# Chunk attention on one Trainium2 core: probabilities by values as three float32r products of high and low parts

## The chip, the cores and the metric

The kernel runs on one core of a Trainium2 chip. The metric is the time of one execution on the device in microseconds (us); the number given for a kernel is the median of several executions. The profile is of one execution, whose own time stands beside it.

## What is computed

Two layers of a streaming encoder, x of 256 frames by 2048 features. Each layer has three groups of heads from one input projection: chunk attention (8 heads of 128), gated linear attention (4 heads), attention into 256 memory tokens (4 heads). The change touches the chunk attention alone:

```python
scores = jnp.einsum('bnqhd,bnkhd->bnhqk', qc, k_band) * (Dh ** -0.5)
scores = jnp.where(valid, scores + bias, NEG_INF)
p = jax.nn.softmax(scores, axis=-1)
out = jnp.einsum('bnhqk,bnkhd->bnqhd', p, v_band)      # probabilities by values
...
y = jnp.concatenate([y_a * silu(a_z), y_b * silu(b_z), y_m * silu(m_z)], axis=-1)
x = layer_norm(alpha * x + y @ w_out, ln_g, ln_b)
```

With 256 frames in chunks of 64 and eight chunks to the left, each frame attends to all frames up to the end of its own chunk. The kernel works in two halves of 128 frames: the first half sees keys 0 to 127, the second keys 0 to 255. So one head's probabilities by values are a product over keys 0 to 127 for all 256 frames (128 x 256) and one over keys 128 to 255 for the second 128 frames (128 x 128).

## The kernel before, in words

**Weights and products.** All projections are a stream of weight pieces (128 x 1024 floats as a rule, 128 x 528 in a part of the value projection). `piece` (L140) loads one into `raw`, and `parts` (L126) splits it: ScalarE (ACT) copies it to float32r, `wh`, and VectorE (DVE) subtracts that from `raw` for the rest, `wl`. TensorE (PE) then makes three float32r products for each of four pairs of k-tile and frame half (`as_products`, L258): high by high, low by high, high by low, twelve matmuls a piece. `raw`, `wh` and `wl` have four buffers each (pool `wp`, L86), so the `wh` of a piece reuses the buffer of the piece four before, and its cast can start only when PE has read that one.

**Attention heads.** `a_head` (L540) is a generator. It issues query by key products as plain float32 matmuls into a PSUM bank, adds the bias and takes the maximum on DVE, the exponential on ACT, scales by the reciprocal sum on DVE, and hands the probabilities `s` to `turned` (L520), which transposes 32 x 32 blocks on DVE and goes through DRAM by POOL's DMA queue into `pT`. Then it yields 9 units of time, and after that issues the values product: two plain float32 matmuls from `asv` (values) and `pT` (L566, L567), and a copy of the bank to `yr` on ACT. A plain float32 matmul appears in the profile as two PE instructions.

`m_head` (L571), the memory heads, already uses the form that the change brings to `a_head`: it splits `pT` into `ph` and `pl` by `parts(..., placed_here)`, yields 2, and issues three float32r products of 128 x 256 for each half of the memory.

**What sets the order.** `tick` (L52) is called once for each piece of weights that PE works through (a fraction of a unit for the narrow pieces). It takes steps of the generators whose time has come: heads start when one of two or three places among the active ones is free, and one step that yields is taken per tick; a generator that ends frees its place within the same tick, and the next starts at once. PE, SP (DMA queue of the weights) and POOL issue in the order in which the code is written (L49). ACT and DVE are ordered by the language's scheduler before the run: the splits of weight pieces have a high priority (`AHEAD`, 4000), and what is marked `placed_here` (L122) stays behind everything that was written before it on its engine. Each engine runs its instructions strictly in that order.

`scratch` (L107) hands out tiles from eight buffers (pool `sc`, L89).

Of the kernel before, what the change touches and what calls it, by code (L numbers as in the profile page):

```python
# [9 lines left out]
F32R = mybir.dt.float32r  # L10
# [8 lines left out]
P = 128  # L19
# [17 lines left out]
def hybrid_trunk_kernel(  # L37
# [59 lines left out]
    def nm(s):  # L97
        uid[0] += 1
        return f"{s}_{uid[0]}"

    def mm(o, l, r, start, stop):
        pe.matmul(o, l, r, start=start, stop=stop, skip_group_check=True)  # L102

    def bank():
        return psa.tile([P, 512], F32, name=nm("bk"), tag="bk")

    def scratch(shape, dtype=F32):  # L107
        return sc.tile(shape, dtype, name=nm("sc"), tag="sc")

    def small(shape, tag, bufs=1):  # L110
        return sm.tile(shape, F32, name=nm(tag), tag=tag, bufs=bufs)
# [14 lines left out]
    def parts(hi, lo, src, keep=lambda ins: ins):  # L126

        keep(act.copy(hi, src))  # L128
        keep(dve.tensor_tensor(lo, src, hi.bitcast(F32), op=ALU.subtract))  # L129
# [390 lines left out]
    def turned(n, *todo, order="p b (g j) -> p g b j"):  # L520

        homes = []
        for _, src in todo:
            blocks = scratch([P, 4, n])
            dve.transpose(blocks.rearrange(order, j=32), src.rearrange("p (g b j) -> p g b j", b=4, j=32))  # L525
            homes.append(drm.tile([P, 4, n], F32, name=nm("home"), tag=f"home{n}"))
            pool.dma_start(homes[-1], blocks)  # L527

        def reads():
            for (dst, _), home in zip(todo, homes):  # L530
                for b in range(4):
                    pool.dma_start(dst[b * 32:(b + 1) * 32], home[:, b].rearrange("(a i) n -> i a n", a=4))  # L532
            return
            yield

        side.append((reads(), now[0] + 2))
# [3 lines left out]
    def a_head(h, load_bias, bias, q, k, asv, y):  # L540

        pb = bank()
        pv = pb.rearrange("p (a j) -> p a j", j=32)
        mm(pv[:, 0:4], q[:, 0:128], k[:, 0:4], True, True)
        mm(pv[:, 4:12], q[:, 128:256], k, True, True)
        s = scratch([P, 384])
        dve.scalar_tensor_tensor(s, pb[:, :384], SCALE, bias[h], op0=ALU.mult, op1=ALU.add)  # L547
        mx = small([P, 2], "mx", 4)
        zs = small([P, 2], "zs", 4)
        own = (slice(0, 128), slice(128, 384))  # L550
        for t in range(2):
            dve.tensor_reduce(mx[:, t:t + 1], s[:, own[t]], AX.X, ALU.max, negate=True)  # L552
        for t in range(2):
            act.activation(s[:, own[t]], s[:, own[t]], AF.Exp, bias=mx[:, t:t + 1], accum_out=zs[:, t:t + 1])  # L554
        dve.reciprocal(zs, zs)
        for t in range(2):
            dve.tensor_scalar(s[:, own[t]], s[:, own[t]], zs[:, t:t + 1], None, op0=ALU.mult)
        pT = tp.tile([P, 4, 96], F32, name=nm("pT"), tag="pT")
        turned(96, (pT, s))
        yield 9  # L560
        if h < 4:
            load_bias(h + 4)
        po = bank()
        v0 = 528 + h * P
        pv, pov = pT.rearrange("p a (g j) -> p g a j", j=32), po[:, :256].rearrange("p (t a j) -> p t a j", t=2, j=32)
        mm(pov, asv[:, 0, v0:v0 + P], pv[:, 0:2], True, False)  # L566
        mm(pov[:, 1], asv[:, 1, v0:v0 + P], pv[:, 2], False, True)  # L567
        act.copy(y, po[:, :256])
        yield 2

    def m_head(h, q, mk, mv, y, laid):  # L571

# [94 lines left out]
    def wo_pieces(l, n):  # L667

        if n < 3:
            return [w512[l, G_WO + n, pc] for pc in range(8)]  # L670
        return [[w256[l, i, pc // 2][:, pc % 2 * 512:pc % 2 * 512 + 512] for i in range(2)] for pc in range(8)]
# [143 lines left out]
    for l in range(L):  # L815
# [63 lines left out]
        asv = per.tile([P, 2, 1552], F32, name=nm("asv"), tag="asv")  # L879
# [17 lines left out]
        home = drm.tile([P, 2, 64], F32, name=nm("home"), tag="home64")  # L897
# [17 lines left out]
        def load_bias(h):  # L915
            bias[h] = hd.tile([P, 384], F32, name=nm("bias"), tag="bias", bufs=4)
            sp.dma_start(bias[h], relw[l, h])
# [20 lines left out]
        for half in range(2):  # L938
            q, k = (hd.tile([P, 4, T], F32, name=nm("qk"), tag="qk", bufs=4) for _ in range(2))
            laid = staged(G_AQ0 if half == 0 else G_AQ1, xq, yraw[3], lambda src, at, q=q: placed_here(act.copy(at(q), src)))  # L940
            load_res(half * 2)
            if half == 0:
                load_bias(2)
            laid += staged(G_AK0 if half == 0 else G_AK1, xq, k, None)
            if half == 0:
                load_bias(3)
            load_res(half * 2 + 1)
            if half == 0:
                values(776, 512)
            else:  # L950
                values(1288, 264)
                mq = staged_queries()
            finish(laid)
            kv = k.rearrange("p x y -> p (x y)").rearrange("p (ta g j) -> p g ta j", g=4, j=32)
            gens.append([a_head(half * 4 + h, load_bias, bias, q[:, h], kv[:, h], asv, yraw[1 + half][:, h]) for h in range(4)])
            waiting.extend(gens[-1])
# [35 lines left out]
        for n in range(WO_N):  # L992
# [3 lines left out]
            src = wo_pieces(l, n)  # L996
# [141 lines left out]
```

## Time and profile before

| | us |
|---|---|
| median of 3 runs (897.84 to 900.17) | 899.92 |
| the profiled execution, own time | 899.75 |
| its span, first to last instruction | 898.0 |
| PE busy (matmul) | 889.1 |
| DVE busy | 613.7 |
| ACT busy | 478.0 |
| POOL busy | 230.9 |

The span is what the trace covers; 1.75 us of the execution's own time lie outside it. A matmul row's duration is from its start to its modelled end, and matmuls overlap: what a matmul costs PE is the distance from its start to the next one's start. In a timeline row, `x4` means four instructions merged, and the first number is the start of the first. "PEld" is the weight load of PE, which runs beside matmuls.

### The profile page before, as it was taken

How to read it: one execution, taken by the hardware profiler on the slowest of the kernel's cores; microseconds unless marked ns; L12 is line 12 of the kernel's file. 1: busy time of each engine (PE TensorE's matmuls, PEld its weight loads, DVE VectorE, ACT ScalarE, POOL GpSimd, SP SyncE). 2: the span in 40 equal slices, each digit the busy share in tenths (PEclk: the TensorE clock that was granted, in tenths of full speed). 3: DMA queues.
4: the chain of work that ended last, by engine and by line, in shares of the span. 5: the costliest groups of instructions: out<-in, count | busy, mean ns of one | idle time of the engine just before them, and what ended most of it. 6: DMA issues, size and time to landing. Idle time of an engine off the chain costs nothing.

```text
span 898.0 us, 13829 instructions
## 1 busy us (share of the span) xinstructions
PE 889.1 (99%) x4663; PEld 743.6 (83%) x4663; DVE 613.7 (68%) x893; ACT 478.0 (53%) x686; POOL 230.9 (26%) x431
## 2 busy tenths in 40 slices
PE   9999999999999999999999999999999999999997
PEld 7888988888988888888888788888888888888885
DVE  6766568757477666665595687896565758676766
ACT  6643574555446565543465544754744457565440
POOL 0022103114315353410033221231061334342300
PEclk9999999999999999999999999999999999999998
DMA  9987779967989797975689879697489887978752
GB/s 301 318 264 223 223 244 263 272 195 226 266 259 242 238 279 228 297 254 193 225 267 270 229 203 291 192 290 219 144 235 290 244 265 232 271 237 275 219 183 93
DMA packets 166086, 216.88 MB, mean 242 GB/s; under 512 B 25232, under 2 KB 143376, under 8 KB 166016
## 3 DMA queue, kind: packets, MB, share of 16 engines
q1 hardware_dynamic: 148256, 173.29, 63.7%
q0 software_dynamic: 17472, 42.33, 16.2%
q8 instruction: 36, 0.59, 0.3%
q10 hardware_dynamic: 288, 0.39, 0.1%
q14 instruction: 34, 0.28, 0.1%
HBM read 194.78 MB, written 21.10 MB: 240 GB/s over the span
## 4 chain that ended last, share of the span: by engine, by line
PE 71%; issue 13%; DMA 9%; DVE 3%; POOL 2%; ACT 1%; SPq 0%; DVEq 0%; POOLq 0%; ACTq 0%
PE acc L102 65%; PE bk L102 6%; DMA zT<-home 2%; DMA home<-sc 2%; DMA xT<-home 2%; DMA raw<-w 2%; DVE wl L129 1%; DMA qk<-home 1%; DMA res<-memT 1%; DMA gb<-ln_b 1%; POOL home L527 0%; POOL xT L532 0%; DMA pT<-home 0%; POOL qk L532 0%; DVE sc L525 0%
## 5 line engine op out<-in xcount | busy, mean ns | idle before, releaser
L102 PE MATMUL acc<-wh,x 128*128 128x512 f32 (+2 forms) x2516 | 748.4, 381 | 0.2 <-ACT wh L128 0.2
L102 PEld LDWEIGHTS acc<-wh,x 128*128 128x128 f32 x2516 | 460.9, 188 | 87.1 <-ACT wh L128 1.0
L129 DVE TENSOR_TENSOR wl<-raw,wh 128x1024 fp32r<-128x1024 f32 (+3 forms) x321 | 368.0, 1151 | 203.0 <-ACT wh L128 196.8
L128 ACT CAST wh<-raw 128x1024 fp32r<-128x1024 f32 (+3 forms) x321 | 318.1, 995 | 336.5 <-PE acc L102 185.7
L102 PE MATMUL acc<-wl,x 128*128 128x512 f32 (+2 forms) x1258 | 476.3, 379 | 1.4 <-DVE wl L129 1.3
L102 PEld LDWEIGHTS acc<-wl,x 128*128 128x128 f32 x1258 | 236.0, 188 | 48.1 <-DVE wl L129 3.5
L527 POOL DMA_DIRECT2D home<-sc x76 | 42.5, 560 | 436.0 <-DVE sc L525 423.1
L532 POOL DMA_DIRECT2D pT<-home x96 | 52.4, 552 | 24.8 <-PE acc L102 8.8
L532 POOL DMA_DIRECT2D qk<-home x64 | 34.9, 553 | 35.5 <-DMA home<-sc 25.2
L532 POOL DMA_DIRECT2D zT<-home x48 | 26.1, 551 | 19.0 <-DMA home<-sc 13.4
L525 DVE STREAM_TRANSPOSE sc<-sc 128x512 f32<-128x512 f32 (+1 forms) x38 | 24.9, 667 | 3.7 <-ACT sc L974 3.0
L532 POOL DMA_DIRECT2D yr<-home x48 | 26.3, 555 | 4.2 <-DMA home<-sc 3.2
L554 ACT ACTIVATE sc<-sc,mx 128x128 f32<-128x128 f32 (+1 forms) x32 | 14.4, 449 | 13.0 <-DVE mx L552 13.0
L525 DVE STREAM_TRANSPOSE sc<-acc 128x512 f32<-128x512 f32 x28 | 18.3, 690 | 4.4 <-PE acc L102 4.3
L547 DVE SCALAR_TENSOR_TENSOR sc<-bk,bias 128x384 f32<-128x384 f32 x16 | 8.6, 538 | 10.8 <-PE bk L102 10.8
L128 ACT CAST x<-sc 128x512 fp32r<-128x512 f32 x20 | 12.3, 618 | 5.3 <-DVE sc L508 2.7
L532 POOL DMA_DIRECT2D xT<-home x24 | 13.2, 552 | 6.5 <-DMA xT<-home 5.3
L129 DVE TENSOR_TENSOR x<-sc,x 128x512 fp32r<-128x512 f32 x20 | 13.5, 684 | 1.4 <-ACT x L128 1.4
L102 PEld LDWEIGHTS bk<-pT,asv 128*128 128x128 f32 x64 | 11.8, 189 | 1.8
L102 PE MATMUL bk<-qk,qk 128*128 128x128 f32 (+1 forms) x64 | 13.1, 326 | 0.0
L676 DVE SCALAR_TENSOR_TENSOR res<-res,acc 128x512 f32<-128x512 f32 x15 | 9.6, 681 | 5.0 <-PE acc L102 5.0
L102 PE MATMUL bk<-pT,asv 128*128 128x256 f32 (+1 forms) x64 | 13.0, 326 | 0.0
(208 smaller groups left out, 508.6 us busy)
## 6 DMA issues: line engine op xcount, KB each, us to landing
raw<-w SPq DMA_DIRECT2D x387, 256.0 KB, 4.6
raw<-w SPq DMA_DIRECT2D x62, 512.0 KB, 4.5
home<-sc POOLq DMA_DIRECT2D x60, 256.0 KB, 4.4
raw<-w SPq DMA_DIRECT2D x32, 388.0 KB, 5.0
raw<-w SPq DMA_DIRECT2D x32, 264.0 KB, 3.5
qk<-home POOLq DMA_DIRECT2D x64, 64.0 KB, 5.4
raw<-w SPq DMA_DIRECT2D x32, 124.0 KB, 4.9
bias<-relw SPq DMA_DIRECT2D x16, 192.0 KB, 4.3
```

What stands on the lines that cost most here:

```text
L102: pe.matmul(o, l, r, start=start, stop=stop, skip_group_check=True)
L128: keep(act.copy(hi, src))
L129: keep(dve.tensor_tensor(lo, src, hi.bitcast(F32), op=ALU.subtract))
L525: dve.transpose(blocks.rearrange(order, j=32), src.rearrange("p (g b j) -> p g b j", b=4, j=32))
L527: pool.dma_start(homes[-1], blocks)
L532: pool.dma_start(dst[b * 32:(b + 1) * 32], home[:, b].rearrange("(a i) n -> i a n", a=4))
L547: dve.scalar_tensor_tensor(s, pb[:, :384], SCALE, bias[h], op0=ALU.mult, op1=ALU.add)
L554: act.activation(s[:, own[t]], s[:, own[t]], AF.Exp, bias=mx[:, t:t + 1], accum_out=zs[:, t:t + 1])
L676: dve.scalar_tensor_tensor(r, r, ALPHA, acc, op0=ALU.mult, op1=ALU.add)
```

## The change

The generator of a head splits its 128 x 256 part of the probabilities (`pv[:, 0:2]`) and its 128 x 128 values of the first half (`asv[:, 0, ...]`) into high and low float32r parts, each pair in one scratch tile, by four more instructions that are placed in program order: two casts on ACT and two subtractions on DVE. It then yields 1 and issues three float32r products of 128 x 256 in place of one plain float32 product. The 128 x 128 part over keys 128 to 255 stays a plain float32 product. The last `yield 2` is gone: the generator ends with the product, so a head lasts 9 + 1 units where it lasted 9 + 2, and the request for the next bias comes one unit later.

```diff
         yield 9
+        v0 = 528 + h * P
+        pv = pT.rearrange("p a (g j) -> p g a j", j=32)
+        ph, pl = split(scratch([P, 512], F32R), 256, pv[:, 0:2], "p (t a j) -> p t a j", t=2, j=32)
+        vh, vl = split(scratch([P, 256], F32R), P, asv[:, 0, v0:v0 + P], "p n -> p n")
+        yield 1
         if h < 4:
             load_bias(h + 4)
         po = bank()
-        v0 = 528 + h * P
-        pv, pov = pT.rearrange("p a (g j) -> p g a j", j=32), po[:, :256].rearrange("p (t a j) -> p t a j", t=2, j=32)
-        mm(pov, asv[:, 0, v0:v0 + P], pv[:, 0:2], True, False)
-        mm(pov[:, 1], asv[:, 1, v0:v0 + P], pv[:, 2], False, True)
+        mm(po[:, :256], vh, ph, True, False)
+        mm(po[:, :256], vl, ph, False, False)
+        mm(po[:, :256], vh, pl, False, False)
+        mm(po[:, P:256].rearrange("p (a j) -> p a j", j=32), asv[:, 1, v0:v0 + P], pv[:, 2], False, True)
         act.copy(y, po[:, :256])
-        yield 2
+
+    def split(home, n, src, shape, **kw):
+
+        hi, lo = home[:, :n], home[:, n:]
+        parts(hi.rearrange(shape, **kw), lo.rearrange(shape, **kw), src, placed_here)
+        return hi, lo
```

The order that comes out of it moves at every head. Three pieces of it follow, all at the values product of the first head of the first layer; the second layer has the same rows there with other numbers. A number behind `wh_` or `wl_` (one higher) names a piece of weights; the pieces run in the order of their numbers.

PE before. `bk_2074` is the first head's values product, `acc_2002` the projection that runs around it:

```order
L102 MATMUL acc_2002<-wh_2042,x_265 128x512 x2
L102 MATMUL acc_2002<-wl_2043,x_265 128x512
L102 MATMUL bk_2074<-pT_1715,asv_686 128x256
L102 MATMUL bk_2074<-pT_1715,asv_686 128x128
L102 MATMUL acc_2002<-wh_2079,x_350 128x512 x2
L102 MATMUL acc_2002<-wl_2080,x_350 128x512
```

PE with the change, where `sc_2072` holds `ph` and `pl`, `sc_2075` holds `vh` and `vl`, and `bk_2109` is the query by key product of the fourth head:

```order
L102 MATMUL acc_2002<-wh_2079,x_350 128x512 x2
L102 MATMUL acc_2002<-wl_2080,x_350 128x512
L102 MATMUL bk_2103<-sc_2072,sc_2075 128x256 x3
L102 MATMUL bk_2103<-pT_1715,asv_686 128x128
L102 MATMUL bk_2109<-qk_1025,qk_1024 128x128
L102 MATMUL bk_2109<-qk_1025,qk_1024 128x256
L102 MATMUL acc_2002<-wh_2129,x_350 128x512 x2
```

The values product has moved one piece later, behind the piece 2079, and the fourth head's query by key product follows it at once.

ACT before. `sc_2025` are the scores of the third head, whose exponential waits for the maximum `mx_2027` from DVE; the pieces behind 2079 are 2102, 2140, 2159, 2182:

```order
L128 CAST wh_2159<-raw_2158 128x1024
L568 COPY yr_1021<-bk_2074 128x256
L128 CAST wh_2182<-raw_2181 128x1024
L554 ACTIVATE sc_2025,zs_2028<-sc_2025,mx_2027 128x128
L554 ACTIVATE sc_2025,zs_2028<-sc_2025,mx_2027 128x256
L128 CAST wh_2201<-raw_2200 128x1024
```

ACT with the change; the pieces behind 2079 are now 2129, 2148, 2171, 2190:

```order
L128 CAST wh_2171<-raw_2170 128x1024
L128 CAST wh_2190<-raw_2189 128x1024
L554 ACTIVATE sc_2025,zs_2028<-sc_2025,mx_2027 128x128
L554 ACTIVATE sc_2025,zs_2028<-sc_2025,mx_2027 128x256
L128 CAST sc_2072<-pT_1715 128x256
L128 CAST sc_2075<-asv_686 128x128
L573 COPY yr_1021<-bk_2103 128x256
```

The two casts of the split stand behind the cast of piece 2190, which takes the buffer of piece 2079, and behind the third head's exponentials.

DVE before, from the third head's maximum on (`sc_2037` are the blocks of its transposition, `sc_2123` the scores of the fourth head):

```order
L552 TENSOR_REDUCE mx_2027<-sc_2025 128x1 x2
L129 TENSOR_TENSOR wl_2183<-raw_2181,wh_2182 128x1024
L555 RECIPROCAL zs_2028<-zs_2028 128x2
L557 TENSOR_SCALAR sc_2025<-sc_2025,zs_2028 128x128
L557 TENSOR_SCALAR sc_2025<-sc_2025,zs_2028 128x256
L525 STREAM_TRANSPOSE sc_2037<-sc_2025 128x3x4x32
L547 SCALAR_TENSOR_TENSOR sc_2123<-bk_2120,bias_1422 128x384
```

DVE with the change:

```order
L552 TENSOR_REDUCE mx_2027<-sc_2025 128x1 x2
L129 TENSOR_TENSOR wl_2191<-raw_2189,wh_2190 128x1024
L555 RECIPROCAL zs_2028<-zs_2028 128x2
L557 TENSOR_SCALAR sc_2025<-sc_2025,zs_2028 128x128
L557 TENSOR_SCALAR sc_2025<-sc_2025,zs_2028 128x256
L525 STREAM_TRANSPOSE sc_2037<-sc_2025 128x3x4x32
L129 TENSOR_TENSOR sc_2072<-pT_1715,sc_2072 128x256
L129 TENSOR_TENSOR sc_2075<-asv_686,sc_2075 128x128
```

The two subtractions of the split stand where the addition of the fourth head's bias stood, behind all of the third head's softmax; the rows ahead of them are the same as before.

## Prediction

> **What bounds the kernel now.** First the page's busy times and its slices.
>
> ```profile
> PE 889.1 (99%) x4663; PEld 743.6 (83%) x4663; DVE 613.7 (68%) x893; ACT 478.0 (53%) x686; POOL 230.9 (26%) x431
> PEclk9999999999999999999999999999999999999998
> ```
>
> PE is busy for 99% of the span at the full granted clock until the last slice. Busy alone proves little, since matmuls overlap, so the second view is the list of waits of PE:
>
> ```profile
> PE acc L102 <- DVE wl L129: 1.3, 3, 0.8
> PE bk L102 <- DVE eps L814: 1.1, 1, 1.1
> PE bk L790 <- DVE nt L755: 0.9, 1, 0.9
> PE bk L102 <- ACT nparts L791: 0.3, 1, 0.3
> PE acc L102 <- ACT wh L128: 0.2, 1, 0.2
> ```
>
> This is the whole list: 3.8 us in 898. No head's product waits for anything. So the time is the sum of what PE issues, and a change pays or costs in two ways only: by the PE time of its matmuls, and by any place where PE begins to wait. A wait isn't made up later, because no stage has PE time to spare.
>
> **What the matmuls cost.** The timeline of PE around the first head's values product, and around a memory head's:
>
> ```profile
> 206.24 0.62 PE L102 MATMUL acc<-wh,x 128*128 128x512 f32 x2
> 206.69 0.39 PE L102 MATMUL acc<-wl,x 128*128 128x512 f32 x1
> 206.92 0.81 PE L102 MATMUL bk<-pT,asv 128*128 128x256 f32 x4
> 207.49 0.71 PE L102 MATMUL acc<-wh,x 128*128 128x512 f32 x2
> 208.04 0.40 PE L102 MATMUL acc<-wl,x 128*128 128x512 f32 x1
> ...
> 210.32 0.62 PE L102 MATMUL acc<-wh,x 128*128 128x512 f32 x2
> ...
> 337.78 0.89 PE L102 MATMUL bk<-sc,mv 128*128 128x256 f32 x6
> 338.51 0.63 PE L102 MATMUL acc<-wh,x 128*128 128x512 f32 x2
> ```
>
> The four instructions of the two plain products take 207.49 - 206.92 = 0.57 us, and the next triple is 0.10 late (0.55 from `wh` to `wl` instead of 0.45): 0.67 in all. By columns, two thirds are the 128x256 part, 0.45. Three float32r products of 128x256 take half of 338.51 - 337.78, or 0.36. Gain: 0.45 - 0.36 = 0.09 by rounded rows; since the 0.10 may belong to whichever product stands last, which stays, I take 0.07 and keep 0.05 to 0.09. Times 16 heads: **-1.1 us** (-0.8 to -1.4).
>
> The Trainium skill ("FP8 and Floating Point Precision", TensorE Precision Notes) counts four passes for a true float32 product. By it the change would save one pass in four, 0.12 us of these rows a head, or 1.9 us in all; the rows show less, and the sum goes by the rows.
>
> **What the split costs on ACT and DVE.** Each head adds two casts and two subtractions; the nearest rows:
>
> ```profile
> L128 ACT CAST sc<-pT 128x256 fp32r<-128x256 f32 x16 | 5.7, 405 | 1.5 <-DMA pT<-home 1.5
> L129 DVE TENSOR_TENSOR sc<-pT,sc 128x256 fp32r<-128x256 f32 x16 | 6.0, 413 | 0.1
> L496 DVE SCALAR_TENSOR_TENSOR x<-yT,ng,x 128x128 fp32r<-128x128 f32 x16 | 4.5, 345 | 0.0
> ```
>
> The 128x256 cast takes 0.41, its subtraction 0.41, the 128x128 subtraction at most 0.35, the 128x128 cast less than 0.41. So some 0.75 us per head on each engine, 12 us in all on engines that are 47% and 32% idle: nothing by itself. What counts is where in the queue they stand, since PE now waits for their result, where it read `pT` and `asv` directly before.
>
> **Where PE will wait.** In the order with the change, the first head's split stands on ACT behind the cast of piece 2190. That cast takes the buffer of piece 2079, and 2079 is the very piece that PE works through just ahead of the values product. So ACT comes to the split only when PE is already at the product. Behind that cast also stand the third head's two exponentials. Before, the cast at the same place, and the exponentials:
>
> ```profile
> 206.89 1.05 ACT L128 CAST wh<-raw 128x1024 fp32r<-128x1024 f32 x1 [0.20 <-PE acc L102]
> ...
> 210.30 1.06 ACT L128 CAST wh<-raw 128x1024 fp32r<-128x1024 f32 x1 [1.96 <-PE acc L102]
> 211.72 0.40 ACT L554 ACTIVATE sc<-sc,mx 128x128 f32<-128x128 f32 x1 [0.37 <-DVE mx L552]
> ...
> 212.52 0.19 ACT L554 ACTIVATION_READ_ACCUMULATOR sc<-sc,mx 128x1 f32 x1
> ```
>
> And DVE from that maximum on:
>
> ```profile
> 211.42 0.60 DVE L552 TENSOR_REDUCE mx<-sc 128x1 f32<-128x128 f32 x2
> 211.94 1.21 DVE L129 TENSOR_TENSOR wl<-raw,wh 128x1024 fp32r<-128x1024 f32 x1
> 213.07 0.16 DVE L555 RECIPROCAL zs<-zs 128x2 f32<-128x2 f32 x1
> 213.26 0.55 DVE L557 TENSOR_SCALAR sc<-sc,zs 128x128 f32<-128x128 f32 x2
> 213.84 0.58 DVE L525 STREAM_TRANSPOSE sc<-sc 128x384 f32<-128x384 f32 x1
> 214.35 0.52 DVE L547 SCALAR_TENSOR_TENSOR sc<-bk,bias 128x384 f32<-128x384 f32 x1
> ```
>
> DVE has no gap in these rows, and the queue ahead of the split is the same with the change; so they keep these times. Now the new order. PE no longer has the values product at 206.92, starts piece 2079 there and is through after 2.73 us (210.32 - 207.49, less the 0.10): at 209.65 it wants the product. ACT casts 2190 from 209.65 to 210.7, waits for the maximum, does the exponentials until 212.7, then the two casts until 213.4. The first product (`vh`, `ph`) can run then, but the second needs the low part of the values, and DVE has both subtractions behind the transposition: the row at 214.35 is where they start, 0.41 and 0.35 make 215.1, and a load of weights (0.19, PEld's mean) 215.3. Without a wait the second product would start 0.12 after 209.65. The difference is 5.5; rows of one DVE queue overlap by a tenth, so **5.4 us**. Bounds: 3.8 if the casts alone decided (213.4 + 0.19), 6.2 if the low parts came a row later.
>
> The second layer has the same rows, and the same order with the change:
>
> ```profile
> 648.64 0.81 PE L102 MATMUL bk<-pT,asv 128*128 128x256 f32 x4
> ...
> 656.08 0.52 DVE L547 SCALAR_TENSOR_TENSOR sc<-bk,bias 128x384 f32<-128x384 f32 x1
> ```
>
> 656.08 + 0.76 + 0.19 - (648.64 + 2.73 + 0.12) = 5.5 again. Two places: **+10.8 us** (7.6 to 12.4). Behind the product ACT holds its copy, the fourth head's exponentials and the next weight cast; PE then has four pieces in hand, 10.9 us, and this chain takes under 5, so no second wait follows.
>
> At the other fourteen heads I went through the same order. The tightest: the fourth head of a layer, whose split stands behind a cast that is released 4.2 us of PE's work ahead of the product (one narrow piece, one full), and the seventh, 3.9 us ahead (a full piece and two heads' products, as three heads' products now stand in a row). The chain there is 1.05 + 1.2 + 0.41 + 0.35 = 3.0 us, so about 1 us is left over. Elsewhere the split is released three pieces or more ahead. ACT also gets four more table loads (1.28 us each), none ahead of a product that is due. I cost these at nothing; the cover is that 1 us.
>
> **The clock.** In the trace PE never stops in mid-kernel, so its clock after a stop is seen only at the ends.
>
> ```profile
> 889.00:892.00 3.00, 1.79 (x6) 0.52 (x4) 2.73 (x13) 0.55 (x2) 0.00 (x0) 1.00 0.00 0
> 892.00:895.00 3.00, 0.90 (x3) 0.41 (x3) 1.24 (x2) 1.27 (x2) 0.00 (x0) 0.64 0.58 211
> L102 PE MATMUL bk<-zeros 128*128 128x128 f32 x14 | 3.4, 432 | 1.1 <-DVE eps L814 1.1
> L102 PE MATMUL bk<-qk,qk 128*128 128x128 f32 x32 | 6.1, 272 | 0.0
> 5.52 0.40 PE L102 MATMUL acc<-wl,x 128*128 128x256 f32 x2
> ```
>
> In the first two rows the third column is PE busy and the third from the end the granted clock. With PE busy 1.79 of 3 us, then 0.90, it fell from 1.00: a mean of 0.64 is 1.00 for 0.8 us and 0.50 for the rest. At the start the 128x128 float32 products ran long (432 against 272 ns), and after 4.5 us of work (1.05 to 5.5) full speed was there: 0.40 for two of 128x256. So a stop of 5.4 us, with one product of 0.12 in it, should halve the clock, and the way back costs at most half of 4.5 us: 0 to 2.2 us a place. Part of the way back may fall into the stop, so I take 1.6; two places **+3.2 us** (0 to 4.4).
>
> The Trainium skill ("TensorE: Matmul & The Clock Gate", Part 1: The HAM clock gate) gives a free-running window of about 3.4 us, one idle one of which halves the clock and one busy one restores it. That speaks against this change more strongly than its own four instructions do: by that rule the place would lose, as an estimate, 0.8 to 2.5 us beyond the stop. The rows above agree with a fall within some 3 us.
>
> **Sum**, against the profiled execution's 899.75 (0.17 under the median of 899.92, so the median serves as well): 899.75 - 1.1 + 10.8 + 3.2 = **912.7 us**.
>
> **Rivals.**
>
> *The stops come, the clock holds.* For it: no row shows a fall in mid-kernel; against it: the row of 0.64. 899.75 - 1.1 + 10.8 = 909.5.
>
> *More heads wait.* The 1 us of cover at the fourth and seventh heads is thin, and a `pT` that lands late holds weight casts behind the split, which it could not do before. For it: the memory heads' casts already wait 1.5 us for `pT` in the row above. Some 3 us more over both layers: 916.
>
> *No wait at all (the other side).* If the low parts were ready by 209.8, PE would wait for nothing, and 899.75 - 1.1 = 898.6 would be left, not slower. The mechanism is the early cast of `ph` and `vh`, and it decides if ACT and DVE ran 5.4 us ahead of the rows above. Against it: the ACT cast ahead waits for PE itself.
>
> **How the numbers follow.** Forecast 912.7: 0.55. Clock holds, 909.5: 0.22. More heads wait, 916: 0.15. No wait, 898.6: 0.08. The range leaves the last out and takes in the bounds: low 899.75 - 1.4 + 7.6 + 0 = 906; high 899.75 - 0.8 + 12.4 + 4.4 + about 2 for other heads = 918. 0.3% (2.7 us) is about what a measurement can tell from no change: slower by more 0.91, within 0.07 (most of the last rival), faster 0.02.
>
> **What would show it.** The waits of PE: two new ones, `bk` on L102 for a subtraction of L129, about 5.4 us in total with the first product between (part of it put down to the cast of L128), near 209.7 and 656 plus the delay so far; the rest of the list as before. PE's timeline: `bk<-sc` three in 0.36 us where it doesn't wait. The slices' PEclk: a digit below 9 after each stop. The prediction is wrong if a stop is under 3.8 us (something ahead of the split on DVE was earlier than in the rows), if there are more than two, or if the products of other heads take longer than 0.6 us.

## The result, and the profile with the change

| | before | with the change |
|---|---|---|
| median, us (four runs each) | 900.04 (897.84 to 901.35) | 920.14 (918.14 to 921.45) |
| profiled execution, own time | 899.75 | 919.11 |
| span | 898.0 | 917.3 |

The change makes the kernel slower: ratio 1.0228, 95% interval 1.0212 to 1.0245. The forecast was 912.7 with a range of 906 to 918: the direction was right, the size was not, and the time lies above the range.

First PE's busy time and its clock by slices, as the page shows them:

```profile
PE 895.6 (98%) x4679; PEld 747.3 (81%) x4679; DVE 623.2 (68%) x925; ACT 491.2 (54%) x722; POOL 230.7 (25%) x431
PEclk9999999998999999999999999999999999999999
```

ACT has 13.2 us more work and DVE 9.5, near the forecast of 12 on each. PE's busy time grew by 6.5 us, though its matmuls are cheaper; the slow clock after the stops, which stretches matmuls, is the likely reason: a kernel with the same matmuls and no stop (the last one of experiment 8) has 887.2. The list of PE's waits says where to look:

```profile
PE bk L102 <- ACT sc L128: 8.4, 4, 3.5
PE bk L102 <- DVE sc L129: 4.1, 4, 1.1
```

These two lines are new and have **four** places each (the second number); the forecast had two. The other lines of the list are those of before, give or take some tenths. Two of the four places are the first heads. PE's timeline there, in the first layer, and the ACT and DVE rows that release it:

```profile
209.50 0.39 PE L102 MATMUL acc<-wl,x 128*128 128x512 f32 x1
213.34 0.58 PE L102 MATMUL bk<-sc,sc 128*128 128x256 f32 x1 [3.46 <-ACT sc L128]
215.07 0.80 PE L102 MATMUL bk<-sc,sc 128*128 128x256 f32 x2 [1.15 <-DVE sc L129]
...
218.23 0.63 PE L102 MATMUL acc<-wl,x 128*128 128x512 f32 x1
...
219.28 0.40 PE L102 MATMUL acc<-wl,x 128*128 128x512 f32 x1
...
219.98 0.39 PE L102 MATMUL acc<-wl,x 128*128 128x512 f32 x1
```

```profile
209.70 1.04 ACT L128 CAST wh<-raw 128x1024 fp32r<-128x1024 f32 x1 [1.67 <-PE acc L102]
...
213.00 0.29 ACT L128 CAST sc<-asv 128x128 fp32r<-128x128 f32 x1
```

```profile
214.74 0.28 DVE L129 TENSOR_TENSOR sc<-asv,sc 128x128 fp32r<-128x128 f32 x1
```

This is the forecast stop row for row: ACT gets its buffer from PE at 209.7, the split's casts end at 213.3, the low parts at 215.0. In the second layer PE waits 3.47 and 1.14 us at the same place. What the stop does to the clock is in the columns of the windows (third column PE busy, third from the end the granted clock):

```profile
209.00:212.00 3.00, 0.89 (x4) 0.38 (x3) 3.00 (x6) 1.23 (x2) 1.66 (x3) 1.00 0.82 268
212.00:215.00 3.00, 0.58 (x1) 0.29 (x1) 2.93 (x8) 1.29 (x6) 0.19 (x1) 0.53 0.62 165
215.00:218.00 3.00, 2.93 (x10) 2.65 (x11) 0.41 (x2) 0.37 (x1) 3.00 (x6) 0.50 0.63 188
218.00:221.00 3.00, 3.00 (x13) 2.40 (x12) 2.14 (x7) 1.12 (x5) 3.00 (x7) 0.83 0.45 112
```

The other two places are the **fourth heads**. In the second layer, PE's last instruction ahead of the product and the products:

```profile
697.75 0.39 PE L102 MATMUL acc<-wl,x 128*128 128x512 f32 x1
699.13 0.39 PE L102 MATMUL bk<-sc,sc 128*128 128x256 f32 x1 [0.99 <-ACT sc L128]
700.42 0.79 PE L102 MATMUL bk<-sc,sc 128*128 128x256 f32 x2 [0.91 <-DVE sc L129]
...
704.33 0.40 PE L102 MATMUL acc<-wl,x 128*128 128x512 f32 x1
```

And ACT, whose casts of weights stand ahead of the split:

```profile
693.21 1.05 ACT L128 CAST wh<-raw 128x1024 fp32r<-128x1024 f32 x1 [4.77 <-DMA raw<-w]
...
697.52 1.05 ACT L128 CAST wh<-raw 128x1024 fp32r<-128x1024 f32 x1 [2.99 <-DMA raw<-w]
698.48 0.40 ACT L128 CAST sc<-pT 128x256 fp32r<-128x256 f32 x1
698.78 0.29 ACT L128 CAST sc<-asv 128x128 fp32r<-128x128 f32 x1
```

Here ACT doesn't wait for PE's buffer, as at the first head: for 7.8 us it waits for **weights that have not landed**. In the first layer it is the same, shorter (2.49 and 1.53 us on ACT). The trace of before had the sign of it. ACT around the fourth head's product of the first layer, and that product:

```profile
235.84 1.05 ACT L128 CAST wh<-raw 128x1024 fp32r<-128x1024 f32 x1 [1.21 <-DMA raw<-w]
241.00 1.05 ACT L128 CAST wh<-raw 128x1024 fp32r<-128x1024 f32 x1 [4.11 <-DMA raw<-w]
```

```profile
240.31 0.81 PE L102 MATMUL bk<-pT,asv 128*128 128x256 f32 x4
```

ACT sat idle for up to 4.11 us for weights, and PE went through its product at 240.31 all the same, since it had pieces in hand and the product read `pT` and `asv`. With the change the product reads what ACT and DVE make, behind those casts.

### The profile page after: what moved, and what is told of

The parts are those of the page before. It is cut to its first block, busy times and chain, and to the rows that moved or that the text cites. A ratio compares the mean times of both kernels' runs of the same rounds, so it can differ in the third digit from the quotient of the medians.

```text
span 917.3 us, 13997 instructions
## 1 busy us (share of the span) xinstructions
PE 895.6 (98%) x4679; PEld 747.3 (81%) x4679; DVE 623.2 (68%) x925; ACT 491.2 (54%) x722; POOL 230.7 (25%) x431
## 4 chain that ended last, share of the span: by engine, by line
PE 72%; issue 12%; DMA 7%; DVE 4%; ACT 3%; POOL 1%; SPq 0%; DVEq 0%; ACTq 0%; POOLq 0%
PE acc L102 66%; PE bk L102 6%; DMA raw<-w 5%; DMA xT<-home 2%; DVE wl L129 1%; ACT wh L128 1%; DMA qk<-home 1%; ACT sc L466 1%; DVE sc L525 1%; POOL xT L532 0%; DMA home<-sc 0%; ACT yr L461 0%; POOL qk L532 0%; POOL home L527 0%; DVE sc L129 0%
## 5 line engine op out<-in xcount | busy, mean ns | idle before, releaser
L102 PE MATMUL bk<-sc,sc 64*64 64x64 f32 (+1 forms) x240 | 14.9, 243 | 12.5 <-ACT sc L128 8.4
L102 PEld LDWEIGHTS bk<-sc,sc 64*64 64x64 f32 (+1 forms) x240 | 11.3, 149 | 16.2 <-ACT sc L128 10.1
L554 ACT ACTIVATE sc<-sc,mx 128x128 f32<-128x128 f32 (+1 forms) x32 | 14.3, 449 | 12.9 <-DVE mx L552 12.8
```

## The experiments

The **theory** after the result: the loss is PE's waiting for the split, in two kinds of places. At the first heads the split stands behind a cast that waits for PE itself; at the fourth heads behind casts that wait for late weights, because the DMA engines are full there. The **rivals**: the added work on ACT and DVE holds up the weights; or the fourth heads' wait belongs to ACT's own work. Each median below stands beside runs of the kernel before that were made with it, and the ratio is to these; the kernel before had medians of 899.0 to 899.6 there and 900.04 beside the change, so medians of different experiments can be compared to about 1 us.

**1. The split made, but not used.**

```diff
-        mm(po[:, :256], vh, ph, True, False)
-        mm(po[:, :256], vl, ph, False, False)
-        mm(po[:, :256], vh, pl, False, False)
-        mm(po[:, P:256].rearrange("p (a j) -> p a j", j=32), asv[:, 1, v0:v0 + P], pv[:, 2], False, True)
+        pov = po[:, :256].rearrange("p (t a j) -> p t a j", t=2, j=32)
+        mm(pov, asv[:, 0, v0:v0 + P], pv[:, 0:2], True, False)
+        mm(pov[:, 1], asv[:, 1, v0:v0 + P], pv[:, 2], False, True)
```

> The order and the four split instructions of the change stay, but the product reads the probabilities and values themselves, as before, so nothing waits for the split. Theory (the loss is PE waiting for the split, at the first and the fourth head of each layer, and the clock that follows): 900, within 1.5, no wait of PE beyond the 3.8 us of before, full clock throughout. Rival (12 us more work on each of ACT and DVE hold up the weight casts, wherever PE waits): the loss stays in good part, 905 to 920, with waits for wh or wl.

Measured: 898.76 against 899.38, ratio 0.9994 (0.9982 to 1.0006). PE's new order and the extra work on ACT and DVE cost nothing that can be seen, so the loss hangs on PE's reading the results. One thing is not as the expectation says: PE, SP and POOL keep the order of the change, but ACT and DVE don't. With no product waiting for it, the split of the first head moved behind the next weight cast (in the first layer that cast starts at 214.74, the split at 215.70). That the split doesn't hold up weights in the change's own order is seen in the change's list of waits: 1.8 us for `wh` and `wl` together, 1.5 before. With both, the first rival falls.

**2. The fourth head plain.** Its product reads `pT` and `asv` again, and its split is left out.

```diff
+        if h not in (3,):
...
+        if h in (3,):
+            pov = po[:, :256].rearrange("p (t a j) -> p t a j", t=2, j=32)
+            mm(pov, asv[:, 0, v0:v0 + P], pv[:, 0:2], True, False)
+            mm(pov[:, 1], asv[:, 1, v0:v0 + P], pv[:, 2], False, True)
+        else:
...
```

> Only the fourth head of each layer goes back to the plain product; its place in the order stays. Theory (the casts ahead of its split wait for weights from memory, and the product waits behind them): the two waits of about 1.8 and 2.4 us and the clock fall of about 1.6 us go, and 0.14 us of saving: 920.1 - 5.7 = 914.4, between 913.5 and 915.5, with first-head stops of 5.4 us as they are. Rival (PE would be late there anyway, because the weights are late): 918 to 920, with waits for wh or wl in place of the split's.

Measured: 913.66, ratio 1.0157 (1.0136 to 1.0179), 6.5 us under the change. PE's list now has two places for the split, not four:

```profile
PE bk L102 <- ACT sc L128: 6.9, 2, 3.5
PE bk L102 <- DVE sc L129: 2.3, 2, 1.1
PE acc L102 <- DVE wl L129: 1.2, 3, 0.5
```

No wait for `wh` or `wl` came in place of the fourth heads' (the 1.2 us for `wl` are no more than before the change, 1.3): PE had its weights, and only the product stood behind the queue. The order of all other instructions is that of the change.

**3. Work for PE in the stop.** Against the kernel of experiment 2:

```diff
+            for _ in range(16 if h == 0 else 0):
+                mm(po[:, 384:], ident, ident, True, True)
             mm(po[:, :256], vh, ph, True, False)
+            for _ in range(6 if h == 0 else 0):
+                mm(po[:, 384:], ident, ident, True, True)
```

> As the kernel with the plain fourth head, but in the first head's stop PE does 22 idle products of the identity by itself (16 before the first product, 6 behind it; an addition to the computation, its result unread). Theory (half clock after each stop costs some 2 us): the stop lasts as long, the clock stays at 1.00, and the kernel is 4 us below the one with the plain fourth head: 910.4, between 909.5 and 911.5. Rival (the clock costs nothing at these places, or the idle products only push the rest back): equal to the kernel with the plain fourth head or slower, 914 to 917.

Measured: 907.72, ratio 1.0089 (1.0070 to 1.0108), under the range that was expected: 5.9 us less than experiment 2 by medians, 3.6 by the two profiled executions (912.67 and 909.08). The first stop in PE's timeline:

```profile
209.24 0.40 PE L102 MATMUL acc<-wl,x 128*128 128x512 f32 x1
209.47 3.73 PE L102 MATMUL bk<-ident 128*128 128x128 f32 x32
213.10 0.39 PE L102 MATMUL bk<-sc,sc 128*128 128x256 f32 x1
...
214.83 0.50 PE L102 MATMUL bk<-sc,sc 128*128 128x256 f32 x2
...
217.88 0.39 PE L102 MATMUL acc<-wl,x 128*128 128x512 f32 x1
```

The stop is as long (213.10 - 209.24 = 3.86 us to the first product, 3.84 in the change). But from the last `wl` ahead of it to the third one behind it go 217.88 - 209.24 = 8.64 us, where the change takes 219.98 - 209.50 = 10.48. So **1.84 us of this stop** are the clock's, and they are saved by work that nobody reads: the granted clock is 1.00 in all windows of 3 us from 209 to 221. The same reckoning in the second layer gives 670.16 - 659.38 = 10.78 in the change and 664.56 - 655.92 = 8.64 here, so 2.14. Together that is 4.0 us, which is what was expected; why the medians differ by 5.9 is open.

**4. A pause behind the product.** A head again lasts two units longer (one part of the change undone):

```diff
         act.copy(y, po[:, :256])
+        yield 2
```

> One part of the change undone: a head again pauses for two pieces behind its product, so that the fourth head's product stands later in the order, four pieces behind the weight cast that stands ahead of its split, not two narrow ones. Theory (fourth head waits for the lateness of casts, first head unaffected): 914.3, between 913.3 and 915.5, both first-head stops as before and none at the fourth head. Rival (the fourth head's wait belongs to the late weights, wherever its product stands): 918 to 921.

Measured: 938.94, ratio 1.0430 (1.0401 to 1.0459): far from both. The fourth heads' waits are gone, as expected; but PE's list has new ones, of which neither theory had spoken:

```profile
PE acc L102 <- ACT x L128: 6.5, 3, 4.0
PE acc L102 <- DVE x L129: 2.0, 3, 0.8
```

```profile
354.64 0.50 PE L102 MATMUL bk<-sc,mv 128*128 128x256 f32 x2 [1.58 <-ACT sc L128]
```

All later heads end later. The first memory head's product (it reads a split as well, before and after the change) now follows the very piece whose buffer the cast ahead of its split waits for, and the operands `x` of the layer's last groups come late. The first heads' stops are there as before, so the pause exchanges the fourth heads' waits for worse ones. The whole of PE's list is 24.8 us longer than before the change; the rest of the 39 us was not taken apart.

**5. Splitting earlier, three ways.** The first keeps a head's old length (7 + 2 + 2 units), the second has the product four units behind the split (7 + 4), the third five (7 + 5):

```diff
-        yield 9
+        yield 7
...
-        yield 1
+        yield 2
...
         act.copy(y, po[:, :256])
+        yield 2
```

> The split moves three pieces earlier and a head keeps its old length of eleven: split after seven pieces, product two later, two more behind it. In ACT's order the cast ahead of the first head's split then needs a buffer four pieces back, not the one just ahead of the product; but the fourth head has one piece between, and the second memory head's split now stands behind a cast for the buffer of the very piece ahead of its product. Theory (a split that stands behind such a cast stops PE wherever it is): both first-head stops gone (-14 us), stops of 3 to 5 us with the clock at the second memory head of each layer, 2 to 3 us at each fourth head: 911, between 906 and 915. Rival (the stop belongs to the first head's place and an early split heals it): 898 to 901.

> The split after seven pieces, the product four later, the head's end with it: eleven pieces a head as before the change. Every split, those of the memory heads too, then has two pieces or more between the release that its ACT queue waits for and its product. Theory: no first-head stop; with no waits at all 899.4 - 1.1 = 898.3. The fourth head has two narrow pieces between, as in the change, where it waited for late weights; if it does so again, up to 5 us more, 903. Rival (splitting earlier only moves ACT's work ahead of weight casts that then come late): over 905.

> As the kernel with the split after seven pieces, but the product five later: a head lasts twelve pieces. The fourth head gets three pieces between, the second memory head two. Theory (the pieces between decide): 898.3, no wait at the fourth head; at most 2 us at the memory heads. Rival (it is the length of a head that costs, as in the kernel with the pause behind the product, whose heads also last twelve): 905 to 920.

Measured: 921.08 (1.0245, 1.0214 to 1.0276), 905.05 (1.0063, 1.0044 to 1.0083) and 899.31 (1.0000, 0.9984 to 1.0017). In none of the three does PE stop at a first head. The first stops at the second memory head, as expected, and longer than expected at the fourth, where one piece is left between, and at the third of the first layer; its 921.08 lies above what was expected of it. The 905.05 of the second lies 2 us above what the theory allowed and on the edge of the rival's "over 905"; its stops are at its fourth heads alone:

```profile
247.27 0.58 PE L102 MATMUL bk<-sc,sc 128*128 128x256 f32 x1 [2.59 <-ACT sc L128]
...
693.17 0.39 PE L102 MATMUL bk<-sc,sc 128*128 128x256 f32 x1 [2.17 <-ACT sc L128]
```

The third has no wait for a split at all. Its heads last twelve units as those of experiment 4 do, so it isn't the length of a head that cost there. What separates these kernels is, first, how many pieces PE still has between the release that ACT's queue ahead of a split waits for and the product behind it:

| kernel | first head | fourth head | lowest of the memory heads | stops |
|---|---|---|---|---|
| the change | 0 | 2 (3 in the second layer) | 2 | first, fourth |
| pause behind the product | 0 | 4 | 0 | first, memory |
| split 7, product 9, pause | 4 | 1 | 0 | fourth, memory, third of the first layer |
| split 7, product 11 | 6 | 2 | 4 | fourth |
| split 7, product 12 | 7 | 3 | 2 | none |

Zero stops PE wherever it stands. Above zero the count alone doesn't decide. Two stop PE at the fourth head and not at a memory head; three stop it at the fourth head of the change's second layer and not in the last kernel of the table; and the seventh head of the change, which the table leaves out, has one piece and two other heads' products between and doesn't stop. At the fourth something else is late.

**6. Fewer bytes of weights.**

```diff
-                sp.dma_start(raw.rearrange("p k n -> p (k n)"), src)
+                sp.dma_start(raw[:, 0], src[:, :n])
+                raw = raw[:, 0:1].to_broadcast([P, kp, n])
```

> The change as it is, every instruction of ACT, DVE and PE in the same order, but each weight piece of 1024 columns fetches only its first half and uses it twice (half of the weights is left out), so weights land earlier. Theory (the fourth head's product waits for casts that wait for weights from memory; the first head's stop waits for PE's own release of a buffer): the fourth head's two waits and their clock fall go, some 5.7 us, the first-head stops of 5.4 us and their half clock stay: 914.5, between 912 and 915.5. Rival (the fourth head waits for ACT's own work, the landing of the probabilities or a buffer that PE holds): 918.5 to 921, waits at the fourth head as they were.

Measured: 917.99, ratio 1.0205 (1.0185 to 1.0224), the fourth heads' waits as they were. The kernel leaves out half of each piece that it halves. It tells nothing on the theory, because the edit missed the place. The table of transfers (count, KB each, median us from issue to landing) of the change and of this kernel:

```profile
raw<-w SPq DMA_DIRECT2D x387, 256.0 KB, 4.6
raw<-w SPq DMA_DIRECT2D x62, 512.0 KB, 5.1
```

```profile
raw<-w SPq DMA_DIRECT2D x443, 256.0 KB, 4.3
...
raw<-w SPq DMA_DIRECT2D x6, 512.0 KB, 6.0
```

56 transfers of 512 KB were halved. The pieces at the fourth heads come as two transfers of 256 KB, and those stayed whole.

**7. More traffic at the place,** in the change and in the kernel of experiment 2:

```diff
+    narrow, spared = [], []
...
+            narrow.append(n)
+            if n == 512 and len(narrow) > 1 and narrow[-2] == 264 and narrow.count(264) % 16 == 0:
+                with tc.high_priority(AHEAD):
+                    sp.dma_start(drm.tile([P, 2, 512], F32, name=nm("spare"), tag="spare"), spared[-1][:, :, :512])
             w = piece(src[pc], n, kp)
...
+        spared.append(asv)
```

> The change, and one spare transfer a layer: 1.05 MB of the values written to scratch memory that nobody reads, issued directly ahead of the weights whose casts stand ahead of the fourth head's split. The casts ahead of each split stay the same ones. Theory (the fourth head's product stands behind casts that wait for weights, because the DMA engines are full there): 1.05 MB at some 300 GB/s is 3.5 us of all engines, so those weights land 2 to 3.5 us later in each layer, the fourth head's product too, and layer 0 gets a clock fall as well: 925 to 929, the first-head stops as before. Rival (the fourth head waits for ACT's own work or for PE's buffers): 919 to 921.5.

> The same spare transfer, in the kernel whose fourth heads have the plain product. Theory (the weights are late there anyway, but PE has pieces in hand and only the split's product waits behind them): little more than that kernel's 913.7, 913 to 916. Rival (weights that land later stop PE whatever product stands there): 917 to 921.

Measured: 920.81 (1.0231, 1.0202 to 1.0260) and 915.25 (1.0174, 1.0146 to 1.0203). The transfer was half as large as its expectation says (512 KB a layer, not 1.05 MB), and the first kernel's total speaks for the rival; the second's 915.25 is as the theory had it. Layer by layer the first kernel's profiled execution, at 923.12 the slowest of its four, splits: in the first layer the two casts waited 4.62 and 4.01 us for weights (2.49 and 1.53 in the change) and PE 3.97 at the fourth head (0.44); in the second the weights were less late than in the change (3.12 and 2.68) and PE waited 0.67 (0.99). So PE's wait went up where the weights came later and down where they came sooner, but not for that reason alone: in the first layer one more weight cast (248.66) and a copy (249.61) stand ahead of the split on ACT (250.10), against what was expected. And the spare transfer didn't make the weights later in both layers. Not settled by this pair.

**8. Less traffic at the place.** Eight reads on POOL's queue bring the second half's keys back from scratch memory while these weights are under way. A copy of one column onto itself on POOL, which needs the fourth head's result, now holds them back; the instructions of every other engine keep their order. Done to the change, and to the kernel with the split after seven and the product after eleven units:

```diff
-        side.append((reads(), now[0] + 2))
+        side.append((reads(), now[0] + pause))
...
         act.copy(y, po[:, :256])
+        if h == 3:
+            pool.tensor_copy(y[:, :1], y[:, :1])
...
-            laid += staged(G_AK0 if half == 0 else G_AK1, xq, k, None)
+            laid += staged(G_AK0 if half == 0 else G_AK1, xq, k, None, 2 + 6 * half)
```

> The change with the same order on every engine, but the eight reads that bring the second half's keys back from scratch memory (0.52 MB on POOL's queue) wait behind a copy of one column on POOL that needs the fourth head's result; so they no longer run beside the weights ahead of the fourth head's split. Theory (the DMA engines are full there, and the casts ahead of the split wait for weights): the weights land sooner, most of the fourth heads' waits and the clock fall with them go, 3.5 to 5.5 us of 920.1: 915.5, between 914 and 917, first-head stops as before. Rival (the casts and the split are held by something else than the traffic): 919 to 921.5.

> The same hold on the reads in the kernel that splits after seven pieces with the product four later, whose only waits were at the fourth heads (905.1). Theory: 899, between 898 and 901.5. Rival: 904 to 906.

Measured: 912.57 (ratio 1.0145, 1.0123 to 1.0167) and 898.27 (0.9984, 0.9971 to 0.9997). The first is 7.6 us under the change, more than expected; the second 6.8 under the 905.05 without the hold. The windows ahead of the fourth head in the second layer, the change first (the last two columns are DMA's busy share and GB/s):

```profile
690.00:694.00 4.00, 4.00 (x36) 4.00 (x35) 0.00 (x0) 0.79 (x1) 0.15 (x1) 1.00 1.08 284
694.00:698.00 4.00, 3.76 (x20) 2.71 (x18) 1.23 (x1) 1.01 (x3) 0.00 (x0) 1.00 1.10 295
```

```profile
690.00:694.00 4.00, 4.00 (x35) 3.96 (x34) 1.23 (x1) 2.04 (x3) 0.00 (x0) 1.00 0.86 289
694.00:698.00 4.00, 4.00 (x22) 3.39 (x21) 3.42 (x5) 4.00 (x8) 0.00 (x0) 1.00 0.74 230
```

In the change the DMA engines are taken up all the time there (1.08 and 1.10). With the reads held back they are not (0.86 and 0.74); from 684 to 696 us the weights' queue moved 2.95 MB where it was 1.98; the weights' median from issue to landing over the same time is 5.8 us where it was 8.6, and the split is on time (ACT first, then PE's products of this head, in one row and without a wait):

```profile
691.14 1.05 ACT L128 CAST wh<-raw 128x1024 fp32r<-128x1024 f32 x1 [3.66 <-DMA raw<-w]
...
693.28 1.05 ACT L128 CAST wh<-raw 128x1024 fp32r<-128x1024 f32 x1 [0.81 <-DMA raw<-w]
694.23 0.40 ACT L128 CAST sc<-pT 128x256 fp32r<-128x256 f32 x1
```

```profile
696.48 0.52 PE L102 MATMUL bk<-sc,sc 128*128 128x256 f32 x3
```

With this the theory stands: the same order with less traffic has no wait at the fourth heads. The last kernel is also the only one whose interval lies wholly under the kernel before, by 0.16%, near what a measurement of this kernel can tell; the saving is of the size of that of the matmuls.

## Why the prediction was wrong

**What bounds the kernel: right.** PE's issue, PE's waits and the clock after them account for the loss of the profiled execution to within 1 us (the sum is below); experiment 1 shows that the added work beside PE is free where PE doesn't read it.

**The matmuls, -1.1: right.** Where nothing waits (the last kernel), from the product to the first `wl` behind it:

```profile
244.69 0.52 PE L102 MATMUL bk<-sc,sc 128*128 128x256 f32 x3
...
245.73 0.39 PE L102 MATMUL acc<-wl,x 128*128 128x512 f32 x1
```

That is 1.04 us, where before it was 208.04 - 206.92 = 1.12. The gain is 0.08 a head and 1.3 us in all (forecast 0.07). By medians that kernel gained 899.55 - 898.27 = 1.28; that the two agree so closely is luck, since its interval runs from 0.3 to 2.6 us.

**The stop at the first heads, +10.8: right.** Without a wait the second product would start at 209.50 + 0.23 + 0.12 = 209.85 (0.23 from a `wl` to what follows, 209.47 - 209.24 in experiment 3; 0.12 a product); it started at 215.07, 5.2 us later, forecast 5.4. In the second layer it is 664.96 - 659.73 = 5.2 again.

**The clock there, +3.2: right in kind, a little small.** 1.84 and 2.14 by the traces, forecast 1.6 a stop. By the windows of the first layer the clock is at half from 212.2 (0.53 for a window of 3 us is 0.18 at full) to 219.0 (0.83 is 1.0 at half), 6.8 us. The Trainium skill ("TensorE: Matmul & The Clock Gate", Part 1: The HAM clock gate) has the clock decided by windows of about 3.4 us; two of them are 6.8, and both costs lie within the estimate of 0.8 to 2.5 us a place that hung on it. Stop and clock together were forecast at 14.0. The two kernels of experiment 8 differ in the place of split and product, and by 912.57 - 898.27 = 14.3.

**The other fourteen heads, at nothing: this step failed.** It was put so: "At the other fourteen heads I went through the same order", with the fourth head's cover at about 1 us. The cover was reckoned from the release by PE of the buffer that the cast takes. A cast has a second input, the weights in `raw`, and at the fourth head ACT waits for that one: for 4.77 and 2.99 us in the second layer. The cover by PE's buffers was even larger there, three pieces between (two narrow, one full) and not the two of the first layer, and PE lost more. PE at the fourth head of the first layer:

```profile
247.04 0.39 PE L102 MATMUL acc<-wl,x 128*128 128x512 f32 x1
247.87 0.39 PE L102 MATMUL bk<-sc,sc 128*128 128x256 f32 x1 [0.44 <-ACT sc L128]
249.16 0.50 PE L102 MATMUL bk<-sc,sc 128*128 128x256 f32 x2 [0.91 <-DVE sc L129]
```

Without a wait the second product would start at 247.04 + 0.23 + 0.12 = 247.39: PE lost 1.8 us. In the second layer it is 700.42 - 698.10 = 2.3, and there the clock falls as well: from the second product to the third `wl` behind it go 704.33 - 700.42 = 3.9 us, where at full clock it is 2.3 (0.92 in the last kernel's rows above, and two triples of 0.69), so 1.6 more. Together 5.7 us. By medians the fourth heads are worth 6.5 (experiment 2) or 7.6 (experiment 8). The forecast missed by 919.11 - 912.7 = 6.4 against the profiled execution, 7.4 against the median. In the profiled execution stops of 10.4, clock of 4.0 and fourth heads of 5.7, less 1.3 for the matmuls, make 18.8 of the 919.11 - 899.75 = 19.4 that were lost; the other 0.6 wasn't traced, nor why the fourth heads are worth up to 2 us more by medians than by these rows.

**The rivals.** "More heads wait", 916 at a chance of 0.15, was the right case, with a wrong mechanism (a `pT` that lands late) and half its price. The range took "about 2 for other heads" to its upper end where 6 were needed. The row that gave the warning, ACT idle for 4.11 us by `DMA raw<-w` at the fourth head, was in the trace of before, where it cost PE nothing; the prediction makes no use of it.

## What to carry to other kernels

When an engine that bounds a kernel is made to read what another engine's queue produces, every wait in that queue ahead of the producer can become its wait, also those that were harmless; go through the queue's idle times by their causes, all inputs of each instruction, in the trace of before. Count the work that the bounding engine still holds between the last release that the queue depends on and the new product; where it was zero, PE had to wait in every kernel here that read the split, and where it is small, ask what the DMA engines do at that place. An earlier split with more pieces between made the same change harmless here (899.31), and with one piece fewer between and traffic moved out of the way it gave a small gain (898.27).

## What the runs showed of the hardware that had not been expected

- A stop is paid twice: 5.2 us of it cost another 1.84 us in the first layer and 2.14 in the second, at half clock. The short stops at the fourth heads went both ways: 0.44 and 0.91 us in the first layer left the clock alone, 0.99 and 0.91 in the second halved it. What decides between the two was not tried.
- With eight reads of 64 KB on POOL's queue beside them, weights took 8.6 us from issue to landing in the median (second layer, 684 to 696 us), and 5.8 with the reads held back; by medians the kernel was 7.6 us shorter without them there. A write of 512 KB a layer issued ahead of the same weights moved the total by nothing that can be told (920.81 and 920.14).
